# Larger blocks, one DMA ring and a fixed transfer order in a streaming DoRA matmul

## Chip, cores, metric

One core of one Trainium2 chip. The metric is the device time of one execution in microseconds (us). All runs that are compared as faster or slower are fast (no execution is over 1.5% above the fastest of its kernel).

## The reference, cut to what matters

```python
W_adapted = W + scale * (lora_A @ lora_B)                  # 256 x 256, rank 16
W_final   = W_adapted / sqrt(sum(W_adapted**2, 0) + 1e-8) * m
y = x.reshape(-1, 256) @ W_final                           # x: 16 x 2048 x 256 fp32, y the same
```

This is DoRA: a weight W with a low-rank update, its columns scaled to the lengths m. 33.6 MB of x come in and 33.6 MB of y go out. The weights are small and are prepared once.

## The kernel before

x is cut into blocks of 32 rows per partition (4 MB, the last in two halves), held in five buffers. A block is cast to bf16 by GpSimd, transposed by TensorE, copied from PSUM by VectorE, multiplied by TensorE, and ScalarE writes the result over x in the same buffer. SyncE loads on its own queue; ScalarE issues the stores on another. (Such a queue is also called a ring here: its transfers are worked off in the order in which they were issued, by 16 DMA engines at once. A packet, or descriptor, is the piece of one row that one DMA engine moves at a time.)

```python
for n in range(len(parts)):                      # SyncE: loads
    b = parts[n][0] // CH
    if b >= XBUFS and parts[n][0] % CH == 0:
        nc.sync.wait_ge(sem(f"store{b - XBUFS}"), 16)
    load_x(n)
...
for p in range(NPR):                             # VectorE: one copy for a pair
    nc.vector.wait_ge(sem("turned"), p + 1)
    nc.vector.tensor_copy(out=xt_bufs[p % NXT]..., in_=xt_ps[p % 2][:])
...
nc.scalar.copy(out=x_bufs[...], in_=y_ps[g % 2][:]).then_inc(sem("room"), 1)
if g == NCH - 1 or part_of[g + 1] != n:          # ScalarE: store when a block is done
    nc.scalar.drain().then_inc(sem("done"), 1)
    nc.scalar.wait_ge(sem("done"), n + 1)
    store_y(n)
...
turned(0)                                        # TensorE
with nc.Fori(0, NPR // 2, 1, engines=[PE], ...):
    turned(1); product(0); product(1); turned(0)
```

## Time and profile before

| | before |
|---|---|
| median of 3 runs (range) | 163.81 us (163.71 to 164.13) |
| the profiled execution | 164.71 us, span 163.2 |
| the same kernel profiled again later | 163.92 us, span 162.2 |
| DMA queues' share of 16 engines | 49.0% loads, 47.8% stores |

The profile was of an execution some 0.9 us slower than the usual one. What limits the kernel, and how that is read, is in the prediction. One line that it does not show, a group of instructions (busy us, mean ns of one | idle us before, and what ended it), is the VectorE copy that the change cuts in two:

```profile
L202 DVE COPY xt<-xt_ps 128x1024 f32<-128x1024 f32 x32 | 38.2, 1221 | 88.1 <-PE xt_ps L267 88.0
```

VectorE idles far more than it works.

### The profile page before, as it was taken

How to read it: one execution, taken by the hardware profiler on the slowest of the kernel's cores; microseconds unless marked ns; L12 is line 12 of the kernel's file. 1: busy time of each engine (PE TensorE's matmuls, PEld its weight loads, DVE VectorE, ACT ScalarE, POOL GpSimd, SP SyncE). 2: the span in 40 equal slices, each digit the busy share in tenths (PEclk: the TensorE clock that was granted, in tenths of full speed). 3: DMA queues.
4: the chain of work that ended last, by engine and by line, in shares of the span. 5: the costliest groups of instructions: out<-in, count | busy, mean ns of one | idle time of the engine just before them, and what ended most of it. 6: DMA issues, size and time to landing. Idle time of an engine off the chain costs nothing. (4 is left out here: it accounts for less than half of the span.)

```text
span 163.2 us, 1988 instructions
## 1 busy us (share of the span) xinstructions
PE 105.3 (65%) x786; PEld 85.2 (52%) x786; DVE 47.2 (29%) x44; ACT 63.8 (39%) x67; POOL 62.5 (38%) x39
## 2 busy tenths in 40 slices
PE   1270599789789897898981998619988820892000
PEld 0130577677577775776760867418676610771000
DVE  0429452350532514405230325005051400330000
ACT  3010027548366384473754053900738440062000
POOL 1006381753935738268004940069209003900000
PEclk9999999999999999999998589985899996599755
DMA  5998998998999999999999999999999999998991
GB/s 201 402 498 386 426 474 385 482 418 265 466 426 426 442 410 466 426 394 482 418 426 442 420 426 458 402 458 410 446 414 454 414 446 422 450 442 377 442 430 60
DMA packets 2915, 67.41 MB, mean 413 GB/s; under 512 B 465, under 2 KB 482, under 8 KB 610
## 3 DMA queue, kind: packets, MB, share of 16 engines
q1 hardware_dynamic: 1440, 33.82, 49.0%
q10 hardware_dynamic: 1474, 33.59, 47.8%
q14 instruction: 1, 0.01, 0.0%
HBM read 33.85 MB, written 33.55 MB: 413 GB/s over the span
## 5 line engine op out<-in xcount | busy, mean ns | idle before, releaser
L219 ACT COPY x_sb<-y_ps 128x1024 f32<-128x1024 f32 x64 | 61.9, 1014 | 75.8 <-PE y_ps L281 75.8
L165 POOL CAST xb<-x_sb 128x2048 bf16<-128x2048 f32 x32 | 60.0, 1902 | 79.3 <-DMA x_sb<-in_x_dram 56.0
L281 PE MATMUL y_ps<-w_final,xt 128*128 128x256 bf16 x512 | 64.6, 280 | 12.8 <-PEq L256 12.8
L202 DVE COPY xt<-xt_ps 128x1024 f32<-128x1024 f32 x32 | 38.2, 1221 | 88.1 <-PE xt_ps L267 88.0
L281 PEld LDWEIGHTS y_ps<-w_final,xt 128*128 128x128 bf16 x512 | 48.4, 100 | 28.2 <-issue 19.8
L267 PE MATMUL xt_ps<-identity,xb 128*128 128x128 f32 x264 | 39.1, 309 | 23.1 <-PEq L256 23.1
L267 PEld LDWEIGHTS xt_ps<-identity,xb 128*128 128x128 f32 x264 | 34.9, 161 | 25.8 <-issue 25.6
L198 DVE TENSOR_TENSOR w_final<-wam,rnorm 128x256 bf16<-128x256 f32 x2 | 4.0, 2028 | 0.0
L244 PE MATMUL y_ps<-sq,ones 128*128 128x256 f32 x4 | 2.1, 674 | 1.6 <-DVE sq L187 1.6
L233 PE MATMUL y_ps<-identity,a_nat 128*16 128x128 f32 x2 | 0.6, 397 | 3.6 <-DMA a_nat<-in_lora_A_dram 3.6
L212 ACT ACTIVATE norm<-y_ps,eps_col 128x256 f32<-128x256 f32 x1 | 0.5, 473 | 6.1 <-PE y_ps L244 6.1
L244 PEld LDWEIGHTS y_ps<-sq,ones 128*128 128x128 f32 x4 | 1.2, 323 | 2.3 <-DVE sq L187 2.1
L210 ACT ACT_TABLE_LOAD x1 | 1.3, 1283 | 2.4 <-issue 2.4
L233 PEld LDWEIGHTS y_ps<-identity,a_nat 128*16 128x16 f32 x2 | 0.1, 90 | 3.6 <-issue 3.6
L171 POOL MEMSET xb<- 128x2048 bf16 x1 | 1.8, 1805 | 0.3 <-PE xt_ps L267 0.3
L195 DVE RECIPROCAL rnorm<-norm 128x256 f32<-128x256 f32 x1 | 1.7, 1745 | 0.0
L237 PE MATMUL y_ps<-b_bf,aT 16*128 16x256 bf16 x2 | 0.6, 404 | 1.5 <-DVE aT L180 1.5
L189 DVE COPY m_all<-y_ps 128x256 f32<-128x256 f32 x1 | 0.4, 425 | 3.3 <-PE y_ps L249 3.3
L178 DVE CAST b_bf<-b_nat 16x256 bf16<-16x256 f32 x1 | 0.3, 281 | 3.8 <-DMA b_nat<-in_lora_B_dram 3.8
L249 PE MATMUL y_ps<-m_row,ones 1*128 1x256 f32 x2 | 1.2, 710 | 0.0
L237 PEld LDWEIGHTS y_ps<-b_bf,aT 16*128 16x128 bf16 x2 | 0.1, 106 | 1.9 <-DVE aT L180 1.9
L183 DVE SCALAR_TENSOR_TENSOR wa<-y_ps,w_nat 128x512 f32<-128x512 f32 x1 | 0.7, 692 | 0.8 <-PE y_ps L237 0.8
(13 smaller groups left out, 3.7 us busy)
## 6 DMA issues: line engine op xcount, KB each, us to landing
x_sb<-in_x_dram SPq DMA_DIRECT2D x7, 4096.0 KB, 27.1
out_dram<-x_sb ACTq DMA_DIRECT2D x7, 4096.0 KB, 37.2
x_sb<-in_x_dram SPq DMA_DIRECT2D x2, 2048.0 KB, 29.6
out_dram<-x_sb ACTq DMA_DIRECT2D x2, 2048.0 KB, 20.2
w_nat<-in_W_dram SPq DMA_DIRECT2D x1, 256.0 KB, 2.9
a_nat<-in_lora_A_dram ACTq DMA_DIRECT2D x1, 16.0 KB, 2.6
b_nat<-in_lora_B_dram ACTq DMA_DIRECT2D x1, 16.0 KB, 3.6
m_row<-in_m_dram ACTq DMA_DIRECT2D x1, 1.0 KB
```

The source lines that it names most:

```text
L165: nc.gpsimd.tensor_copy(out=xb_bufs[p % NXB][:], in_=x_bufs[b % XBUFS][:, 2 * c * J : 2 * (c + 1) * J, :],).then_inc(sem("rounded"), 1)
L171: nc.gpsimd.memset(xb_bufs[NPR % NXB][:], 0.0).then_inc(sem("rounded"), 1)
L183: nc.vector.scalar_tensor_tensor(out=wa[:], in0=ab_ps, scalar=float(scale), in1=w_nat[:], op0=ALU.mult, op1=ALU.add).then_inc(dv, 1)
L195: nc.vector.reciprocal(out=rnorm[:], in_=norm[:]).then_inc(dv, 1)
L198: i = nc.vector.tensor_mul(out=w_final[:, t], in0=wam[:, t], in1=rnorm[:])
L202: nc.vector.tensor_copy(out=xt_bufs[p % NXT][:].rearrange("p r t -> p (r t)").bitcast(FP32), in_=xt_ps[p % 2][:],).then_inc(sem("copied"), 1)
L210: nc.scalar.activation(out=warm[:], in_=eps_col[:], func=AF.Sqrt)
L219: nc.scalar.copy(out=x_bufs[b % XBUFS][:, c * J : (c + 1) * J, :], in_=y_ps[g % 2][:]).then_inc(sem("room"), 1)
L244: i = nc.tensor.matmul(n2_ps, ones[:], sq[:, t, :], start=(t == 0), stop=(t == KC - 1))
L249: nc.tensor.matmul(mb_ps, ones[0:1, :], m_row[:], start=True, stop=True).then_inc(pe, 1)
L267: i = nc.tensor.transpose(xt_ps[p % 2][:, j * P : (j + 1) * P], xb_bufs[p % NXB][:, j, :].bitcast(FP32), identity[:],)
L281: i = nc.tensor.matmul(y_ps[h][:, j, :], xt_bufs[p % NXT][:, r : r + P, t], w_final[:, t, :], start=(t == 0 and (j % (J // 2)) == 0), stop ...
```

## The change

The intent: blocks of 64 rows per partition make every row of a transfer 64 KB long; all transfers go on one ring (SyncE's) in one fixed order of loads (L) and stores (S), so that loads and stores never alternate. There are three buffers of 64 KB per partition, the weights' scratch lies in the third one before x arrives there, and the transposed x is kept by half pair.

```diff
-    DJ = 32
+    BLOCKS = [64, 64, 64, 64]
+    STORES = [[64], [64], [64], [16, 16, 16, 16]]
+    RING = "L0 L1 L2 S0 S1 L3 S2 S3 S4 S5 S6".split()
-    XBUFS = 5
+    XBUFS = 3
...
-    w_nat = sb("w_nat", [P, KC, OUT], FP32)        # and the other weight tiles
+    spare = x_bufs[XBUFS - 1]
+    w_nat = spare[:, 0:2, :]
...
+    for what in RING:
+        k = int(what[1:])
+        if what[0] == "S":
+            nc.sync.wait_ge(sem("done"), k + 1)
+            store_y(k)
+            continue
+        if k == XBUFS - 1:
+            nc.sync.wait_ge(sem("dve"), 8)
+        for n in range(len(stores)):
+            if stores[n][0] == k - XBUFS:
+                nc.sync.wait_ge(sem(f"store{n}"), 16)
+        load_x(k)
...
-    for p in range(NPR):
-        nc.vector.wait_ge(sem("turned"), p + 1)
+    for g in range(NCH):
+        p, h = divmod(g, 2)
+        if g >= NXT and (h == 1 or p % 2 == 1):
+            nc.vector.wait_ge(sem("product"), g - NXT + 1)
+        if h == 0:
+            nc.vector.wait_ge(sem("turned"), p + 1)
         nc.vector.tensor_copy(
-            out=xt_bufs[p % NXT]..., in_=xt_ps[p % 2][:],
+            out=xt_bufs[g % NXT]..., in_=xt_ps[p % 2][:, h * F4 : (h + 1) * F4],
```

## The prediction

> **What bounds the kernel now.** I read the page first: the strip of 40 slices, the two DMA queues, the groups of instructions.
>
> ```profile
> span 163.2 us, 1988 instructions
> PE 105.3 (65%) x786; PEld 85.2 (52%) x786; DVE 47.2 (29%) x44; ACT 63.8 (39%) x67; POOL 62.5 (38%) x39
> ...
> DMA  5998998998999999999999999999999999998991
> ...
> q1 hardware_dynamic: 1440, 33.82, 49.0%
> q10 hardware_dynamic: 1474, 33.59, 47.8%
> ...
> L165 POOL CAST xb<-x_sb 128x2048 bf16<-128x2048 f32 x32 | 60.0, 1902 | 79.3 <-DMA x_sb<-in_x_dram 56.0
> ```
>
> No engine is busy for more than 65% of the span, but the DMA row is at 9 or an accidental 8 from the second slice to the last but one. The two queues (q1 carries SyncE's loads, q10 ScalarE's stores) took 49.0 + 47.8 = 96.8% of the sixteen DMA engines' span, which is 158.0 us of 163.2. GpSimd, first of the compute engines to touch a block, waited 56.0 us for loads. The kernel is a stream of 67.4 MB with compute beside it, and only 5.2 us of DMA time per engine is not used.
>
> Is the stream as fast as it can go, or does the mixing of loads and stores slow it? Five stretches answer that. The last three columns are granted TensorE clock, DMA share and GB/s (packets are put down whole, so a share may pass 1):
>
> ```profile
> 4.00:34.00 30.00, 18.39 (x114) 13.95 (x113) 13.63 (x14) 7.77 (x9) 11.39 (x6) 1.00 1.01 437
> 34.00:42.00 8.00, 6.72 (x59) 5.57 (x57) 3.47 (x3) 4.27 (x5) 4.75 (x3) 1.00 0.92 328
> 42.00:134.00 92.00, 71.49 (x560) 58.53 (x560) 27.43 (x24) 46.45 (x48) 40.07 (x22) 0.93 1.00 432
> 138.00:158.00 20.00, 8.33 (x56) 7.06 (x56) 2.45 (x2) 3.85 (x4) 4.77 (x3) 0.76 0.99 424
> 158.00:164.00 6.00, 0.00 (x0) 0.00 (x0) 0.00 (x0) 0.00 (x0) 0.00 (x0) 0.50 0.28 120
> ```
>
> Loads alone (4 to 34) run at 437 GB/s, loads and stores mixed (42 to 134) at 432, stores alone (138 to 158) at 424 with that edge effect. So mixing costs almost nothing. Two stretches do lose: 34 to 42, where the first store (issued at 34.52) joins the loads, and the ragged end after 158.
>
> The trace's records of single DMA packets give the size of each loss. A 32 KB packet takes 1213 ns at the median, load or store, whether the queues alternate or not; a 16 KB one takes 611. The next packet on an engine starts about 4 ns before the last one ends. Three things lie outside those medians:
> - Around 36 to 38.5 us some 25 load packets take 1.3 to 2.9 us instead of 1.21. Summed over loads (mean 1240 against 1213, 896 packets, 16 engines) that is 1.5 us per engine, of which some 0.3 is the ramp at 3 us: a one-off stall of about 1.2 us when the first store starts.
> - The last store's completion increments come at 159.48 to 160.33 us from fifteen engines and at 162.69 from one. That laggard is 0.3 us behind the fifteen at the first store's end and 2.4 behind at the end: about 40 of its 32 KB store packets took some 52 ns more than 1213, only while compute was running, and its loads were normal.
> - The first x packet starts at 3.05 us.
>
> Together: 3.05 + 0.3 ramp + 112 packets x 1.209 + 32 x 0.607 (a 16th of the traffic) + 1.2 stall = 159.4, which is the first of the fifteen; + 0.85 spread + 2.4 laggard = 162.6, and the span ends at 163.2.
>
> **What the Trainium skill says.** "DMA: Bandwidth & Descriptors", section "Issuing engines are not separate DMA queues": DMAs of all issuing engines end on the same 16 DMA engines and interleave. The trace agrees (1213 ns alone or mixed), so moving the stores to SyncE's ring buys no bandwidth. Same page, section "Where 436 GB/s comes from": a ceiling of 435 GB/s. 16 x 32,768 bytes in 1.213 us is 432 here, so at most 0.7% lies above it. Same page, "Why small descriptors are slow (HBM only)": a fixed overhead per packet. Here 2 x 611 - 1213 = 9 ns per packet, far below 1% of 1213. "TensorE: Matmul & The Clock Gate", section on the HAM clock gate: activity releases the throttle, an idle stretch brings it back. Before agrees: from 42 to 134 the granted clock is 0.93, with 0.5 in some 4 us slices near the waits for loads, and a first cycle there takes 12.0 us (cast at 107.46 to last copy at 119.48) instead of some 11.
>
> **The change part by part.**
>
> *64 KB descriptors.* From 602 ns per further 16 KB, a 64 KB packet should take 611 + 3 x 602 = 2417 ns, 2413 of it apart. An engine's share is now 56 of these plus 32 of 16 KB in the four last stores: 135.1 + 19.4 = 154.5, against 112 x 1.209 + 19.4 = 154.8. Gain 0.3 us.
>
> *One ring, fixed order.* It can only lose, by a gap, if the next transfer is issued too late. One block (8.39 MB, 8 packets an engine) takes 8 x 2.413 = 19.3 us. From 3.4 us: L0 lands at 22.7, L1 42.0, L2 61.3, S0 80.6, S1 99.9, L3 119.2, S2 138.5, S3 to S6 143.4, 148.2, 153.1, 157.9 (L a load, S a store). Compute must keep up with that. A cycle of two pairs (16 rows) takes 6.6 us now (ScalarE's copies at 36.87, 43.48, 50.09), so a block of 64 rows takes 26.4, plus about 4.3 us until the first copy of a pair can follow the load.
> - Block 0: 22.7 to about 53. S0 is wanted at 61.3: 8 us spare.
> - Block 1: to about 80. S1 wanted at 80.6: tight if the cycle stays 6.6.
> - Block 2: to about 106. S2 wanted at 119.2: 13 us spare.
> - L3 needs S0's data out (80.6, plus 2 to 3 us for the laggard), wanted at 99.9: 16 us spare.
> - Block 3: load at 119.2 (121.5 on the laggard). Before, the last block's final two pairs took from the cast at 137.23 to the copy's end at 148.1, so 10.9 us for the first store and 6.6 for each further one: 132.4, 139.0, 145.6, 152.2 if the laggard set the landing. They are wanted at 138.5, 143.4, 148.2, 153.1, less about 1.7 us from issue to first packet (1.36 to 3.05 at the start). The last is a few tenths late on fifteen engines and 2 us early on the laggard, which sets the end.
>
> *Copies halved, xt by half pair.* 32 copies of 1221 ns become 64 of roughly 0.65 us (an estimate from half the elements plus a little fixed cost), so VectorE rises from 38 to about 42 us busy: harmless. The first product of a cycle need no longer await the whole pair's copy: TensorE waits 0.69 us there now (the line of products "idle before" in the timeline at 42.41), and the half copy ends while the second eight transposes still run. The new wait of a copy for the product two before it fits under ScalarE's 1.01 us copies. So I expect a cycle of 5.9 to 6.6 us. This makes block 1 and the last store fit; it is not itself on the path that sets the end.
>
> *Weights in the third buffer.* L2's issue waits for w_final, ready at 18.0 us (the product at 14.05 took 3.98). L1 streams until 42, so this is hidden with 24 us to spare. The preparation is otherwise the same.
>
> *What stays open in the sum.* The start stall of 1.2 us: if the second ring's start caused it, it goes; if the first write to HBM did, it comes again around 61. I give each a half: -0.6. The laggard: store time beside compute is about as long as before (61 to 100 and 122 to 150), so I leave its 2.4 us; if its cost is per packet, half of the packets would save about 1 us. I count -0.1 for that chance, net of what a late last store may cost.
>
> Sum: 163.8 - 0.3 - 0.6 - 0.1 = 162.8 us.
>
> **The rivals.**
> 1. *The single ring gaps*, because compute is late for S1 or the last stores, or because the ring drains at a boundary. For it: the fit at 80 and at 152 us is within 1 or 2 us; block 3 starts after 15 us of idle TensorE, so perhaps at clock 0.5, costing 1 us. Against it: in the load-only stretch three boundaries between DMAs (landings at 13.3, 23.0, 32.8) pass without a gap, all 16 engines busy. It would give 164 to 167 us.
> 2. *Stall and laggard both go*, because both belong to the ACT ring. For it: the slow packets are all on q10, and the stall begins 1.6 us after q10's first store. Against it: the laggard's 16 KB stores on the same ring, when compute had ended, were normal, so the ring alone is not the cause; and a store is also the only thing that writes HBM. It would give 163.8 - 0.3 - 1.2 - 2.4 = 159.9, faster by 2.4%.
> 3. *Unmixed reads and writes are faster.* Against it: 1213 ns in every stage. I give it nothing.
>
> **Range and chances.** A clean stream of 67.1 MB cannot be much under 159 us. The middle of the cases (stall back or not, laggard there) is 162.2 to 163.5. Range 161.0 to 164.8. Faster by over 2% means under 160.53, which takes rival 2 whole: 0.13. Slower by over 2% means over 167.1, which takes a gap of 4 us: 0.04. Within 2%: 0.83.
>
> **What would show it.** In the profile after: the DMA row at 9 from slice 2 to the end; 64 KB packets of about 2417 ns; SyncE's wait before L3 long but no slice with low DMA around 61, 81, 100, 119; loads landing near 22.7, 42, 61 and 119; copies to xt of about 0.65 us and cycles of 5.9 to 6.6; the last increments 2 to 3 us apart, or all within 1 us if rival 2 holds. I am wrong if 64 KB packets take more than twice 1213, if the DMA row shows a hole, or if the laggard is gone.

## The result, and the profile after

| | before | after |
|---|---|---|
| median (range), 4 runs each | 163.79 us (163.71 to 164.13) | 165.51 us (165.29 to 165.69) |
| ratio | 1 | 1.0101, 95% interval 1.0081 to 1.0120 |
| profiled execution | span 163.2 (later one 162.2) | span 164.1 |

I had forecast a small gain, 162.8 us with a range of 161.0 to 164.8. The change costs 1% instead, clear of the noise, though at a threshold of 2% the two kernels count as the same. (A ratio is the mean time of one kernel's fast runs over that of the other's of the same rounds, so it is not quite the ratio of the medians.)

The page of the changed kernel, strips of 40 slices in tenths:

```profile
span 164.1 us, 2054 instructions
PE   1440008999899999989989983000003998998400
PEclk9999999999999999999999999655555599999985
DMA  8799969959969989599799979969979988899990
q1 hardware_dynamic: 1728, 67.37, 96.1%
q14 instruction: 2, 0.02, 0.0%
L225 DVE COPY xt<-xt_ps 128x512 f32<-128x512 f32 x64 | 42.7, 689 | 94.8 <-PE xt_ps L288 77.2
```

q1 has all transfers now and took 96.1% of the DMA engines' span (96.8% for the two queues before). The dips of the DMA row to 5 and 6 are not holes: a 64 KB packet is put down whole, so that a slice gets two or one of them per engine. The packet records show every engine with its next packet starting about 4 ns before the last one ends, up to about 159 us, with two exceptions: at the boundary before the last store, near 155 us, several engines wait 0.1 to 0.6 us, and one engine each pauses 0.3 us at 82 and 106 us, where the two packets of q14, the instruction queue, ran. TensorE has a long rest (102 to 126 us) while the fourth load streams.

SyncE's queue, who waited for whom (us in total, times, longest):

```profile
SPq L137 <- ACTq L247: 131.1, 7, 38.4
SPq L131 <- DVE w_final L215: 11.5, 1, 11.5
SPq L131 <- DMA out_dram<-x_sb: 6.2, 1, 6.2
```

SyncE waits 131 us for ScalarE to finish blocks and 11.5 us for w_final. None of it is a loss, but for those tenths before the last store, since the ring still held work.

Five stretches (PE, PEld, DVE, ACT, POOL busy us with counts; then granted clock, DMA share, GB/s):

```profile
18.00:62.00 44.00, 33.83 (x276) 28.58 (x277) 15.95 (x24) 20.78 (x22) 25.97 (x14) 1.00 0.98 413
62.00:102.00 40.00, 35.25 (x303) 29.30 (x300) 16.10 (x25) 25.53 (x27) 18.85 (x11) 1.00 1.02 443
102.00:120.00 18.00, 0.00 (x0) 0.00 (x0) 0.00 (x0) 0.00 (x0) 0.00 (x0) 0.56 0.95 412
120.00:140.00 20.00, 13.28 (x92) 10.99 (x93) 5.35 (x8) 6.00 (x7) 11.21 (x6) 0.72 0.98 422
140.00:155.00 15.00, 12.75 (x111) 10.66 (x108) 5.34 (x8) 9.44 (x10) 5.54 (x3) 1.00 1.00 428
```

From 62 to 102 the ring holds nothing but stores, and TensorE runs for 35 of the 40 us. From 102 to 120 it holds nothing but a load, and TensorE does nothing at all. From 120 on there are stores again, and TensorE again.

Where is the time? The packet records (start, duration and size of every packet, and of the increments that each of the 16 engines writes at the end of a transfer) give the following. "Lag" is how far the last engine's increment is behind the last but one's at the end of the last store. "Stall" is the sum of the excess of slow load packets over the median up to the first store, per engine; it sits in the last few microseconds before that store's data (36 to 39 us before, 58 to 61 after), but for the first profile of the changed kernel, where 0.8 of the 1.36 us is spread over 32 to 57.

```
                         before     before    after     after
                       (1st prof) (2nd prof) (1st)    (2nd prof)
packet, median ns         1213       1213     2418       2418   (32 KB / 64 KB)
stall, us                 1.30       0.86     1.36       1.34
last but one engine ends 160.33     159.84   160.32     160.07
last engine ends         162.69     161.72   163.62     163.61
lag, us                   2.36       1.87     3.31       3.55
```

Fifteen engines end about where they did. The one laggard ends 1 to 2 us later than before, and it alone sets the end. In the changed kernel nearly every 64 KB store packet of that engine between 64 and 100 us takes about 127 ns more than 2418; the last load packet, at 120 us, takes 1036 ns more; its first store packets after that are normal, and from 128 to 131 us on, after TensorE's restart at 125.9, they are slow again; its increments fall back from 0.5 us behind the next engine's (first store) to 1.0 (second), 1.9 (fourth load), 2.6 (third store) and 3.3.

### The profile page after: what moved, and what is told of

Same layout as the page of the kernel before. It is cut to its first block, busy times and chain, and to the rows that moved or that the text cites. A ratio compares the mean times of both kernels' runs of the same rounds, so it can differ in the third digit from the quotient of the medians.

```text
span 164.1 us, 2054 instructions
## 1 busy us (share of the span) xinstructions
PE 99.5 (61%) x786; PEld 81.4 (50%) x786; DVE 48.5 (30%) x76; ACT 63.7 (39%) x67; POOL 62.3 (38%) x39
## 3 DMA queue, kind: packets, MB, share of 16 engines
q1 hardware_dynamic: 1728, 67.37, 96.1%
## 5 line engine op out<-in xcount | busy, mean ns | idle before, releaser
L225 DVE COPY xt<-xt_ps 128x512 f32<-128x512 f32 x64 | 42.7, 689 | 94.8 <-PE xt_ps L288 77.2
L302 PE MATMUL y_ps<-w_final,xt 128*128 128x256 bf16 x512 | 62.6, 274 | 7.4 <-PEq L277 7.4
L288 PE MATMUL xt_ps<-identity,xb 128*128 128x128 f32 x264 | 35.3, 291 | 41.1 <-PEq L277 41.1
L302 PEld LDWEIGHTS y_ps<-w_final,xt 128*128 128x128 bf16 x512 | 47.5, 99 | 21.8 <-issue 14.3
L288 PEld LDWEIGHTS xt_ps<-identity,xb 128*128 128x128 f32 x264 | 32.1, 150 | 42.8 <-issue 42.6
L265 PE MATMUL y_ps<-x_sb 128*128 128x256 f32 x4 | 2.1, 674 | 1.6 <-DVE x_sb L204 1.6
L265 PEld LDWEIGHTS y_ps<-x_sb 128*128 128x128 f32 x4 | 1.2, 323 | 2.3 <-DVE x_sb L204 2.1
L212 DVE RECIPROCAL x_sb<-x_sb 128x256 f32<-128x256 f32 x1 | 1.7, 1744 | 0.0
L270 PE MATMUL y_ps<-x_sb 1*128 1x256 f32 x2 | 1.2, 710 | 0.0
L209 DVE TENSOR_TENSOR x_sb<-x_sb 128x256 f32<-128x256 f32 x2 | 0.8, 421 | 0.0
```

Of the source, the lines that this page charges most:

```text
L209: i = nc.vector.tensor_mul(out=wam[:, t], in0=wa[:, t], in1=m_all[:])
L212: nc.vector.reciprocal(out=rnorm[:], in_=norm[:]).then_inc(dv, 1)
L225: nc.vector.tensor_copy(out=xt_bufs[g % NXT][:].rearrange("p r t -> p (r t)").bitcast(FP32), in_=xt_ps[p % 2][:, h * F4 : (h + 1) * F4],). ...
L265: i = nc.tensor.matmul(n2_ps, ones[:], sq[:, t, :], start=(t == 0), stop=(t == KC - 1))
L270: nc.tensor.matmul(mb_ps, ones[0:1, :], m_row[:], start=True, stop=True).then_inc(pe, 1)
L288: i = nc.tensor.transpose(xt_ps[p % 2][:, j * P : (j + 1) * P], xb_bufs[p % NXB][:, j, :].bitcast(FP32), identity[:],)
```

## The experiments

**Theory A**: the laggard is slow for stores while compute runs; the fixed order put almost all store time beside compute. **Rivals**: B, stores from one ring slow that engine by themselves; C, the 64 KB descriptors do; D, one ring instead of two costs. "WRONG" below means that the result is wrong on purpose.

**Before, profiled again** (no edit).

> The kernel before, unchanged, profiled again, because the profile that I predicted from was of a 164.71 us execution while the median is 163.79. If the difference lies in the laggard DMA engine, its lag at the last store (2.36 us behind the next slowest) should be 1.4 to 1.6 us here in a run of about 163.8; if it lies in the one-off stall at the first store (excess 1.30 us per engine), that should be about 0.4 us. Time 163.8, ratio 1.00.

163.82 us, ratio 1.0003 (0.9968 to 1.0038). The second profile has span 162.2, lag 1.87, stall 0.86 (table above). So of the 0.9 us that my first profile had too much, about half is laggard and half is stall, and neither of my two answers was right alone.

**No compute on x** (WRONG).

```diff
-            nc.sync.wait_ge(sem("done"), k + 1)
+            nc.sync.wait_ge(sem(f"load{stores[k][0]}"), 16)
             store_y(k)
-    (the loops over x of GpSimd, VectorE, ScalarE and TensorE)
```

> The changed kernel's ring with the same eleven transfers in the same order, but no compute on x at all (each store waits for its load; results wrong on purpose). Theory A (the laggard engine is slow only for stores beside running compute): all 16 engines end within 1.2 us, the span falls by about 3 us to 161, time about 162.3. Rival B (stores from one ring, or 64 KB descriptors, slow that engine by themselves): the laggard is again about 3.3 us behind, time about 165. The stall: if it belongs to compute it goes as well (another 1.3 us, time 161), if to the first store's issue or the first write it stays, near 23 or 61 us.

161.51 us, ratio 0.9858 (0.9833 to 0.9883). In the profiled execution (162.15 us, the longest of the four) all 16 engines end between 159.66 and 160.48 us. The page:

```profile
span 160.8 us, 119 instructions
PE   0450000000000000000000000000000000000000
DMA  8699699699699696997997997989979979799997
q1 hardware_dynamic: 1728, 67.37, 98.1%
```

The same transfers in the same order without compute, and the laggard is gone: theory A, against B. The stall stayed: 1.04 us at 58 to 61 us. SyncE had issued the first store at 23.57 us here and at about 52.5 in the changed kernel, whose second profile has 1.34 us at the same place, 58 to 61. So it belongs to the place in the ring where the loads end and the first store starts, not to the store's issue, nor to compute, nor to a second ring.

**32 KB descriptors.** Every 64-row transfer as two of 32 rows.

```diff
+        for r in range(0, BLOCKS[b], 32):
             nc.sync.dma_start(
-                out=x_bufs[b % XBUFS][:, 0 : BLOCKS[b], :], in_=in_dram(x_flat, b)
+                out=x_bufs[b % XBUFS][:, r : r + 32, :], in_=in_dram(x_flat, b)[:, r : r + 32, :]
```

> The changed kernel with every 64-row transfer as two of 32 rows, so 32 KB descriptors, everything else the same. Theory A: packets of 1213 ns, the laggard about 3.3 us behind as in the changed kernel, time 165.5 to 166.0 (0.3 us more packet overhead). Rival C (64 KB descriptors make the laggard worse): the lag falls to about 2.4 us or less and the time to 164.0 to 164.7.

165.03 us, ratio 1.0077 (1.0054 to 1.0101); lag 2.53. The slow store packets lose some 60 ns each, half of 127 for half the bytes, so the steady part does not depend on the descriptor. But the jump at 120 us (1036 ns) is not there: 68 and 61 at most. So rival C is right in part: about 1 us of lag comes with 64 KB descriptors, and saving packet overhead gives back some of it.

**Two rings again.** The stores are issued by ScalarE.

```diff
-        nc.sync.dma_start(
+        nc.scalar.dma_start(
             out=in_dram(out_flat, b)[:, r0 : r0 + cnt, :],
```

> The changed kernel with the stores issued by ScalarE on its own ring as before, same sizes and buffers. Rival D (one ring in a fixed order is what costs): the time falls to 163.8 to 164.5. Theory A: the laggard's loss depends on how many store bytes move beside compute, and mixing spreads stores over a time with less compute or as much; lag 2.4 to 3.3 us, time 164.5 to 165.8. If the block order now lets loads lag, a hole shows in the DMA row and the time grows above 166.

164.21 us, ratio 1.0040 (1.0007 to 1.0072): better than one ring. By the numbers this is D's forecast, and theory A's (a lag of 2.4 to 3.3 us, 164.5 us or more) missed; the trace shows another reason than D's. The rings alternate, so the fourth load lands at 122.8 to 125.7 us instead of 120.5 to 123.5, and ScalarE issues the last stores one compute cycle apart, in the timeline (start us, duration):

```profile
137.80 0.34 ACTq L137 DMA_DIRECT2D out_dram<-x_sb  x1
...
143.91 0.34 ACTq L137 DMA_DIRECT2D out_dram<-x_sb  x1
...
149.99 0.34 ACTq L137 DMA_DIRECT2D out_dram<-x_sb  x1
...
156.06 0.34 ACTq L137 DMA_DIRECT2D out_dram<-x_sb  x1
```

A cycle is 6.1 us and a 16-row store takes 4.9, so from 140 us on the DMA engines run dry between stores:

```profile
140.00:164.00 24.00, 14.51 (x125) 11.92 (x122) 6.37 (x10) 11.21 (x12) 6.84 (x4) 0.93 0.81 341
```

The share is 0.81, and the laggard catches up in the pauses: lag 0.14 us, and fifteen engines end at 161.9 instead of 160.3. The end is then set by when the last store is issued (156.06 us), not by the laggard. The fixed order does keep the tail full; it just pays elsewhere.

**One compute engine at a time** beside the transfers of the run without compute (all WRONG, one execution each). TensorE runs its whole loop on scratch data; ScalarE, VectorE and GpSimd make copies or casts into scratch, back to back, from 42 us. The edits, condensed:

```diff
+    nc.tensor.wait_ge(sem("load1"), 16)          # TensorE: the loop of 256 transposes, 512 products
+    nc.scalar.copy(out=<scratch>, in_=xt_ps[g % 2][:])                    # 64 times
+    nc.vector.tensor_copy(out=<scratch>, in_=xt_ps[g % 2][:, 0:F4])       # 128 times
+    nc.gpsimd.tensor_copy(out=xb_bufs[p % NXB][:], in_=x_bufs[1][...])    # 32 times
```

> The run without compute, plus TensorE alone: from the landing of the second load (42 us) it runs the whole loop of 256 transposes and 512 products on scratch data, some 105 us, free of the other engines (results wrong on purpose). In the changed kernel the laggard was 1.0 us behind the next slowest engine and 1.7 behind the middle one at the end of the second store (103.1 us) and 3.3 at the end. If TensorE's activity (or its many instruction records) is what slows stores on that engine, the lag is 1.5 us or more at 101 us and 2.5 or more at the end. If not, all 16 engines stay within 1.1 us of each other.

> The run without compute, plus ScalarE alone: 64 copies of 128x1024 from PSUM into scratch, from the landing of the second load on (42 to about 108 us; results wrong on purpose). If ScalarE's writes cause the slow stores, the laggard's lag against the middle engine is about 1.7 us at 101 us; if not, within 1.1 us.

> The run without compute, plus VectorE alone: 128 copies of 128x512 from PSUM into scratch from 42 us to about 130 us (results wrong on purpose). If VectorE's copies cause the slow stores, lag about 1.7 us at 101 us; if not, within 1.1 us.

> The run without compute, plus GpSimd alone: 32 casts of 128x2048 from the second block into scratch from 42 us to about 103 us (results wrong on purpose). If GpSimd's casts, which share SBUF with the stores' reads, cause the slow stores, lag about 1.7 us at 101 us; if not, within 1.1 us.

| beside the transfers | time | last but one / last engine | lag |
|---|---|---|---|
| nothing | 161.51 | 160.43 / 160.48 | 0.05 |
| TensorE | 165.29 | 160.10 / 163.46 | 3.36 |
| ScalarE | 161.86 | 159.89 / 160.20 | 0.31 |
| VectorE | 162.77 | 160.92 / 161.09 | 0.17 |
| GpSimd | 161.71 | 159.96 / 160.01 | 0.05 |

TensorE alone makes the whole laggard, with the same 110 to 145 ns a store packet and a jump (1460 ns) at 120 us. The page of that run:

```profile
span 164.0 us, 1811 instructions
PE   1440000000009999999999999999999992000000
q1 hardware_dynamic: 1728, 67.37, 96.2%
```

VectorE's run has two engines about 1 us behind the middle one, from single slow packets, not the steady loss. What this does not separate is TensorE from the mere number of instructions: TensorE issued some 1550 here, ScalarE 64, VectorE 128 and GpSimd 32, and at the 2.5 ns each found below those three would lag 0.3 us at most, no more than the scatter. Whether other engines' instructions cost as much is not tested.

**Work or number of instructions?** TensorE alone again (WRONG), products only: 768 of 256 columns, then 384 of 512 columns.

```diff
-                for j in range(J):
+                for j in range(0, J, 2):
-                    nc.tensor.matmul(y_ps[h][:, j, :], xt..., w_final[:, t, :], ...)
+                    nc.tensor.matmul(y_ps[h][:, j : j + 2, :], xt..., w_final[:], ...)
```

> The TensorE-alone run with products only: 768 of 256 columns (one weight load each) from 42 us on, about 82 us at 107 ns each, no transposes (results wrong on purpose). It is the control of the next run. The lag at the end should be about 3.4 us as with the full loop, if any steady TensorE work will do; if it was the fp32 transposes, it falls under 1 us.

> As the control, but 384 products of 512 columns, so the same array time of about 82 us in half as many instructions (results wrong on purpose). If the slow engine pays per TensorE instruction (fetching them, or writing the profile's records), its 64 KB store packets lose about 60 ns instead of 125 and the lag at the end of the second store falls to about half of the control's. If it pays for the array's activity or the operand reads, both are as in the control.

The stretch of the two stores, first the narrow and then the wide products:

```profile
62.00:100.00 38.00, 38.00 (x351) 34.06 (x349) 0.00 (x0) 0.00 (x0) 0.00 (x0) 1.00 1.02 440
```

```profile
62.00:100.00 38.00, 38.00 (x178) 17.24 (x177) 0.00 (x0) 0.00 (x0) 0.00 (x0) 1.00 1.02 442
```

TensorE is busy all 38 us in both, with half the instructions in the second. The slow packets lose some 125 ns in the first and 60 to 75 in most in the second; the lag at the end is 3.25 against 1.61 us, the times 165.01 and 163.09. So, by one execution of each, the slow engine pays by the number of TensorE instructions, not by the columns streamed or the time that the array is busy. The weight loads, and the bytes they read, are halved with the products, so these runs don't tell a cost of every instruction from one of weight loads alone.

**Taking work off the slow engine.** The last 16-row store is cut by partitions into 0 to 119 and 120 to 127, in the changed kernel and in the one before.

```diff
+        for lo, hi in [(0, 120), (120, P)] if n == len(stores) - 1 else [(0, P)]:
-                out=in_dram(out_flat, b)[:, r0 : r0 + cnt, :], in_=...
+                out=in_dram(out_flat, b)[lo:hi, r0 : r0 + cnt, :], in_=...
```

> The changed kernel, its last 16-row store cut in two: partitions 0 to 119 and 120 to 127, so that the first runs on 15 DMA engines and the second on 8, and the 16th engine has none of it (4.9 us of work less for it). If the laggard is that 16th engine, it ends at about 158.8 us, the eight engines with one packet more at 160.9, and the time falls from 165.5 to about 162.9. If the laggard is one of the eight, it is 0.6 us later: 166.1. If it is one of the seven between, nothing changes: 165.5.

> The kernel before with the same cut in its last 16-row store. If the laggard is the 16th engine there too, its 1.9 us of lag goes, the eight engines end 0.6 us later, and the time falls from 163.8 to about 162.5; otherwise 163.8 to 164.4.

Both got slower than the kernel before: 168.07 us (ratio 1.0276, 1.0252 to 1.0301) and 166.67 us (1.0193, 1.0163 to 1.0222, so whether by over 2% is unclear). In the stretch of the last store, the changed kernel and this one:

```profile
154.00:164.00 10.00, 0.00 (x0) 0.00 (x0) 0.00 (x0) 0.00 (x0) 0.00 (x0) 0.73 0.58 244
```

```profile
154.00:164.00 10.00, 0.00 (x0) 0.00 (x0) 0.00 (x0) 0.00 (x0) 0.00 (x0) 0.76 0.87 236
```

The engines are busy for 0.87 instead of 0.58 of the time and move no more: in the last store the packets take 1.09 us at the median, and half of them 1.0 to 1.5, instead of 0.61 (0.8 at the median in the other kernel). Why is not shown. The packet records do narrow down the laggard, most clearly in the second run: once it has ended its second to last store (at 159.07 and 158.21 us), it moves eight packets of the larger part, each in 611 ns, and then one of the smaller part. So it is one of the eight engines that have both parts, and this cut could not relieve it.

**Does the account fit in size?** More kernels keep the ring, the order, the buffers and the stores, and only land the loads in pieces, so that TensorE starts earlier, beside loads.

```diff
+        for r in range(0, BLOCKS[b], 32):        # 16 in the other
             nc.sync.dma_start(
-                out=x_bufs[b % XBUFS][:, 0 : BLOCKS[b], :], in_=in_dram(x_flat, b)
+                out=x_bufs[b % XBUFS][:, r : r + 32, :], in_=in_dram(x_flat, b)[:, r : r + 32, :]
-            ).then_inc(sem(f"load{b}"), 16)
+            ).then_inc(sem(f"load{b}_{r}"), 16)
```

> The changed kernel unchanged: ratio to before 1.010, lag of the last engine behind the next 3.0 to 3.4 us at the end, with the jump of about 1 us at its last packet of the fourth load (near 120 us) if that is systematic, 2.3 without it.

> Each 64-row load as two of 32 rows with a semaphore each; the cast waits for its half. Compute starts at about 18 us (w_final) instead of 22.6, and beside the fourth load's second half. TensorE beside stores: 62 to about 92 and 120 to 138, some 47 us instead of 70, so by the theory the lag falls by a third (from 3.3 to about 2.2 to 2.5) and the time to about 164.6. If the lag stays at 3.3, the theory of the size is wrong.

> The same with loads of 16 rows (16 KB packets, some 0.5 us more packet overhead for half the traffic). The fourth block can be computed from about 106 us on, so TensorE beside stores is 62 to about 92 and 120 to 134, some 43 us; lag about 2.0 to 2.3 us, time 164.5 to 165.0 with the overhead. Beating the kernel before (163.8) would take a lag under 1.2.

| on one chip, 4 runs each | median | ratio to before | lag |
|---|---|---|---|
| the changed kernel again | 165.66 | 1.0122 (1.0105 to 1.0139) | 3.55 |
| loads in halves | 164.07 | 1.0025 (1.0009 to 1.0042) | 1.92 |
| loads in quarters | 163.46 | 0.9978 (0.9961 to 0.9995) | 1.76 |

The stretches with quarters:

```profile
18.00:62.00 44.00, 40.91 (x337) 34.06 (x336) 18.58 (x28) 26.93 (x28) 26.13 (x14) 1.00 1.01 428
62.00:102.00 40.00, 27.23 (x233) 22.44 (x231) 13.36 (x20) 19.56 (x21) 14.94 (x8) 0.94 1.00 432
102.00:120.00 18.00, 9.66 (x66) 8.33 (x67) 3.90 (x6) 3.86 (x4) 8.60 (x5) 0.67 1.01 431
120.00:140.00 20.00, 15.73 (x136) 13.01 (x134) 6.78 (x11) 11.57 (x12) 8.14 (x5) 1.00 1.01 436
140.00:155.00 15.00, 0.00 (x0) 0.00 (x0) 0.00 (x0) 0.00 (x0) 0.00 (x0) 0.54 1.00 427
```

Read against the same five of the changed kernel: 337 instead of 276 matmuls beside the first loads, 233 instead of 303 beside the first two stores, 66 instead of none beside the fourth load, none instead of 111 beside the last stores. The lag falls by half and the time with it, more than I expected, because the jump at 120 us is mostly gone as well (234 and 54 ns on the last two load packets with halves, 24 ns with quarters). It was there in both executions of the changed kernel (1036 and 888 ns), so it is systematic. With quarters the fixed order beats the kernel before, by 0.2% (which counts as the same), though I had asked for a lag under 1.2 us for that.

These two edits change the loads' packets as well as TensorE's start. The run with 32 KB descriptors is the control: packets as small as with halves (its stores' too), TensorE as late as in the changed kernel, and a lag of 2.53 us against 1.92 (times 1.0077 and 1.0025 of before). So some 0.6 us of the lag goes with the earlier start, and about 1 us with the smaller packets. The stall shrinks with quarters too: slow load packets sum to about 0.5 us per engine before the first store, against 1.0 with halves and 1.34 in the changed kernel run beside them.

To compare sizes I summed over TensorE's matmuls and weight loads after 20 us: each counts with the share of the 16 engines that had a store packet in flight at its start.

```
                          instructions beside stores   lag us   ns each
before (1st, 2nd prof)          690, 741             2.36, 1.87   3.4, 2.5
after (1st, 2nd prof)           987, 997             3.31, 3.55   3.4, 3.6
32 KB descriptors                  988                 2.53        2.6
loads in halves                    770                 1.92        2.5
loads in quarters                  711                 1.76        2.5
TensorE alone                      984                 3.36        3.4
narrow / wide products          996 / 494          3.25 / 1.61   3.3 / 3.3
```

About 2.5 ns for each instruction beside stores explains the four that have no jump; those of the changed kernel have the jump of 0.9 to 1.0 us on top (987 x 2.5 ns = 2.5; + 1.0 = 3.5). It is a rough figure: with their jumps of 1.46 and 1.2 us, TensorE alone and the narrow products would come to 3.9 and 3.7 us, against 3.36 and 3.25 measured. The first profile of before does not fit as well (690 x 2.5 = 1.7 against 2.36), and I take that as the scatter of a single execution.

## Why the prediction was wrong

**Right.** A 64 KB packet takes 2418 ns (I had 2417), VectorE's half copies 0.689 us (0.65), a cycle 6.1 us (5.9 to 6.6). On the first of the 16 engines, transfers ended at 22.6, 42.3, 62.6, 81.9, 101.2, 120.5 and 139.8 us for L0, L1, L2, S0, S1, L3 and S2 (22.7, 42.0, 61.3, 80.6, 99.9, 119.2, 138.5): my numbers, plus the stall of 1.3 us from L2 on. The ring never starved but for some tenths at the last store; the weights in the third buffer were hidden. Block 3's first store was issued at 135.7 and its last at 153.9 us, where I had them ready at 132.4 and 152.2: the load reached its last engine at 123.5 instead of 121.5, and TensorE's clock was 0.72 from 120 to 140. S2 was still in the ring, so only the last store met a gap. So rival 1, gaps, did not happen beyond that, and that unmixed transfers are no faster (rival 3) held as well.

**Failed: the laggard.** The step was "store time beside compute is about as long as before (61 to 100 and 122 to 150), so I leave its 2.4 us". The stretches of time were about as long, but I counted them and not what ran in them: before, loads and stores alternate, so in those stretches only about half of the packet time was stores; in the changed kernel all of it is. TensorE's instructions beside stores went from 741 to 987, and the lag from 1.87 to 3.31 to 3.55 us: 0.6 us of that from the count (246 x 2.5 ns), 0.9 to 1.0 from a jump on the last 64 KB load packet that I did not foresee. The chance that the cost is per packet, for which I had counted a gain, failed too: a slow packet of twice the size loses twice as much (52 ns, then 127).

**Failed: the stall.** I gave it half a chance to vanish (-0.6). It came again, 1.36 us (where the first write was to bring it back, so that half of the guess held), and the run without compute shows it at the first store's start in the ring, without compute. (A second turn from loads to stores, at 118 to 121 us, cost 0.5 us there and 0.1 in the changed kernel.) And in my first profile of before it was larger (1.30) than in the second (0.86).

The same sum with the measured terms: 163.8 - 0.2 (56 packets x 4 ns: 2414 ns apart instead of 2 x 1209) + 0.5 (stall, 1.36 for 0.86) + 1.5 (lag, 3.4 for 1.87) = 165.6, against 165.5 measured. With the first profile's terms for before (1.30, 2.36) it would be 164.7: one profile was too little to size terms of half a microsecond. (A slip without effect: 9 ns of 1213 is 0.7%, not "far below 1%".)

**Rival 2**, that stall and laggard go because both belong to ScalarE's ring, is refuted: both are there on SyncE's ring.

**Open.** Why TensorE's instructions slow one engine is not shown. One guess was that this engine fetches them. The traces speak against it: the pages of the three runs with TensorE alone have no packet on the instruction queue (q14), and yet lags of 3.36, 3.25 and 1.61 us; the changed kernel has two such packets, on other engines than the laggard. The other guess is that it carries records that the profiler writes for each instruction. These runs cannot test that: every timed execution came with its span and clock, so none was certainly unrecorded, and the loss may be smaller or absent in a run without a profiler. The cause of the jump at 120 us is not shown either; it is there (0.9 to 1.5 us, on the laggard alone) in all five profiles that have one ring, 64 KB load packets and a laggard already over 1 us behind at the end of the second store, 0.5 us at most where the wide products left it 0.7 behind, and in no run with smaller load packets (0.3 us at most, with halves).

## What to carry to other kernels

When a stream is limited by its slowest DMA engine, look at the spread of the engines' completion increments, not only at the mean share: here 15 engines idled for the last 3 us. What runs beside a store matters, so an order that keeps loads and stores apart should put the heavy instruction streams beside the loads; landing the loads in 16-row pieces, and waiting for each, did that and was worth 1.3% against the changed kernel, part of it from the smaller packets themselves. And profile the starting point twice before summing terms smaller than the spread of its runs.

## What the Trainium skill lacked or had wrong

- "DMA: Bandwidth & Descriptors", section "Latency and other measured facts", has two engines that are usually slower, with a best guess that is specific to DMAs issued by GpSimd. Here no DMA was issued by GpSimd, and yet one engine was slow, beside stores, in step with the number of TensorE's instructions: a lag of 3.36 us with TensorE alone, 3.25 with products only, 1.61 with half as many, 0.05 without compute.
- No page that I found has the stall at the first store after a run of loads: 0.9 to 1.4 us per engine with packets of 32 and 64 KB, about 0.5 with loads of 16 KB, in the last load packets before it, with one ring or two.
- "DMA: Bandwidth & Descriptors", section "Why a DMA increments its semaphore by 16 and not by 1", says how many engines a DMA uses; the 120 + 8 partition store agrees (15 + 8 increments by engines). It does not say that such a store is slow: its 16 KB packets took 1.09 us at the median instead of 0.61 (0.8 in the kernel before with the same cut).
